# Sparse attention in a pinned order: softmax by single heads, out weight splits at named places, two transposes later, the last unit ahead of the next input

## The chip, the cores and the metric

The kernel runs on one core of a Trainium2 chip. Its time is device microseconds of one execution. Five engines work beside each other, each in its own instruction order: TensorE (PE: matmuls and transposes, into PSUM banks), VectorE (DVE), ScalarE (ACT), GpSimd (POOL) and SyncE (SP, which here issues nearly all loads). TensorE's clock is granted by a throttle; the profile gives it as a share of full speed (1.00 is 2.4 GHz, 0.50 is 1.2 GHz).

## The reference

Four layers over 256 tokens of width 1024, each x -> x + 1/2 FFN_a(x) -> x + Mixer(x) -> x + 1/2 FFN_b(x), every step between two RMS norms with a shift, scale and gate from a conditioning vector. Layers 0 and 3 have native sparse attention (NSA) as mixer, layer 1 stick-breaking and layer 2 differential attention. What matters here of the NSA mixer, for one block of 128 tokens:

```python
s = jnp.einsum('bqgrd,bngd->bgrqn', qb, k_cmp) * scale           # 15 compressed keys
p_cmp = jax.nn.softmax(where(valid, s - slopes * dist, NEG)) * valid
o_cmp = jnp.einsum('bgrqn,bngd->bqgrd', p_cmp, v_cmp)
...                                                             # the selected keys k_g, the window's keys kwb
p_sel = softmax(where(dist >= 0, s_sel - slopes * dist, NEG))
p_win = softmax(where(valid, s_win - slopes * d_int, NEG))
o = g[..., 0:1] * o_cmp + g[..., 1:2] * o_sel + g[..., 2:3] * o_win
return o.reshape(B, Q_BLK, NSA_QW) @ w_out
```

There are 16 heads in 4 groups. `k_cmp` and `v_cmp` come from a small two-layer network over windows of 32 tokens. With 256 tokens all four selection blocks are taken, and the window reaches over all tokens before, so both softmaxes run over all earlier tokens.

## The kernel before

All products are made in three passes of split single precision (hi x hi, lo x hi, hi x lo); each weight is loaded raw by SP (`raw_*`), cast to its high part on ACT (L135, `hi_*`) and its rest is made on DVE (L136, `lo_*`). Raw and split weights sit in rings of a few buffers, so a load waits until an older one has been used.

The NSA mixer is cut into named pieces, and the strings `plan` and `rest` give the order of the pieces. `run` calls them through `pin`, which lets the first TensorE instruction of a piece issue only after the last TensorE instruction of the piece before. So TensorE's order is that of the plan; the order on DVE, ACT and SP is decided by the scheduler from the order and the priorities in which the instructions are written.

There are four units: a (head groups 0 and 1, tokens 0 to 127), b (the same heads, tokens 128 to 255), c and d (groups 2 and 3, the two blocks of tokens). The pieces are:

- `gate`: the product p_g for the three gates, its tanh `gt` on ACT (L864) and its transposes `p_gt` (L867); `q gp part`: chunks of the query product in a bank `p_pr` with two halves, emptied to `qkv` by ACT (L774, even half) or DVE (L772, odd half); `kc`: keys and values for compression.
- `S u rp`: scores `p_s` (L915) of two heads of each of two groups (e is the group, rr the head) and their softmax: a score reduction on DVE (L920) that subtracts the distance and takes the maximum, for all eight rows of the pair; the maxima times the slope (L927); eight exponentials with sums (ACT, L933); reciprocal (L936) and the multiply by the gates (L937); eight multiplies `sc` (L943).
- `T u rp n`: four transposes `p_t` of the probabilities (L951) and a copy `pT` by ACT (L953); `P u rp n`: values times `pT` into the unit's bank `p_o` (L896).
- `hid k`: the first layer of the compression network, two loads `raw_cw` each; after `hid 3` its activation. `cout`: transposes `p_ht`, copy `hT` (L842), `p_kcT` and `p_vc`, which give the compressed keys and values.
- `C u`, `D u`, `E u`: the compressed branch: scores `p_sc` (L966) and softmax `pc`, transposes `p_t<-ident,pc` (L685) with their copies `pT` by ACT or DVE (L631), and the product `p_o<-pT,vc`. `put` moves `p_o` into `yh` and `yl` (L627, L628), the input of the out projection.
- `o h k n`: out projection of token block h with chunk k of the weights (`raw_wo`, `hi_wo`, `lo_wo`), for half n of the columns or both. `out_weight(k)` is called in `o`, where the chunk is first used.

Around it, the main loop calls `body` (the plan), then `post` for token block 0 (norm and residual, L371 to L377), `pre` (norm of the next step's input and its transposes `p_y`, L339), and then `tail` (the rest) with the work of token block 1. Score banks (`mm`) and transpose banks (`tp`) come in pairs, accumulators (`acc`) in fours.

Of the kernel before, what the change touches and what calls it, by code (L numbers as in the profile page):

```python
# [40 lines left out]
def trunk_kernel(ctx, tc, x, c, ada_w, ada_b, norm_g, ffn_w1, ffn_w2, nsa_w_in, nsa_cmp_pe, nsa_cmp_w1,  # L41
# [610 lines left out]
    def softmax_alibi(h, qk, sc, sl, nsl):  # L652


        K, n = 128 * (h + 1), len(qk[0])
        m = small([128, 2 * n], "sm_m")
        per = min(512 // K, n)
        for j0 in range(0, n, per):
            p = [bank("mm", [128, per, K], "p_s") for _ in range(2)]
            for j in range(per):  # L660
                for e in range(2):
                    qT, kT = qk[e][j0 + j]
                    nc.tensor.matmul(p[e][:, j, :], qT, kT[:, :K], start=True, stop=True)
# [28 lines left out]
    class Nsa(Mixer):  # L692
        W = D + 6 * 256 + 48
        plan = """gate; q 0 0; S a 0; q 0 2; S b 0 0; q 0 3; S b 0 1; kc 0 0; S a 1; T a 0 0; T a 0 1; kc 0 1; P a 0 0; P a 0 1;
                  kc 1 0; T b 0 0; T b 0 1; kc 1 1; P b 0 0; T b 0 2; P b 0 1; T b 0 3; q 1 4; P b 0 2; P b 0 3; S b 1 0;
                  q 1 5; S b 1 1; T a 1 0; T a 1 1; hid 0; P a 1 0; P a 1 1; S c 0; hid 1; hid 2; hid 3; T b 1 0; T b 1 1;
# [5 lines left out]
                  put d; o 1 0 1; o 1 1 1; o 1 2 1; o 1 3 1; o 1 4 0; o 1 5 0; o 1 6 0; o 1 7 0; o 1 4 1; o 1 5 1; o 1 6 1; o 1 7 1"""  # L702
# [60 lines left out]
        def q(self, gp, part):  # L763

            self.load_q(gp)
            for r in ((0, 1), (2, 3), (2,), (3,), (0,), (1,))[part]:
                if not r % 2:
                    self.pq = bank("acc", [128, 2, T], "p_pr")
                mm_w(self.pq[:, r % 2, :], self.w[gp], chunk(r))
                j = 4 * gp + r  # L770
                if r % 2:
                    nc.vector.tensor_scalar(self.qT[:, j, :], self.pq[:, 1, :], qscale[:, j:j + 1], None, op0=OP.mult)  # L772
                else:
                    nc.scalar.activation(self.qT[:, j, :], self.pq[:, 0, :], AF.Copy, scale=qscale[:, j:j + 1])  # L774
# [61 lines left out]
        def cout(self):  # L836
# [5 lines left out]
            nc.vector.tensor_copy(hT, p)  # L842
            self.kcmp = work.tile([128, 2, 2, 16], FT, name="kc", tag="kc", bufs=1)
# [15 lines left out]
        def gate(self):  # L859
# [4 lines left out]
            nc.scalar.activation(gt, p, AF.Tanh, scale=0.5)  # L864
            pt = bank("tp", [128, 2, 48], "p_gt")
            for h in range(2):
                nc.tensor.transpose(pt[:, h, :], gt[:, h * 128:(h + 1) * 128], ident[:48, :48])  # L867
            nc.vector.tensor_scalar(self.gates.rearrange("p h a b -> p h (a b)"), pt, 0.5, 0.5, op0=OP.mult, op1=OP.add)

        def o(self, h, k, n=None):  # L870
# [6 lines left out]
            if k not in self.wo:  # L877
                self.wo[k] = self.out_weight(k)
# [3 lines left out]
        class Attend:  # L882


            def __init__(self, nsa, gp, h):
                self.nsa, self.gp, self.h = nsa, gp, h
                self.tok, self.K = slice(h * 128, (h + 1) * 128), 128 * (h + 1)
                self.po, self.sc, self.m, self.t, self.ct = None, {}, {}, {}, {}
# [10 lines left out]
            def S(self, rp, r=None):  # L899
# [3 lines left out]
                if rs[0] == 0:  # L903
# [5 lines left out]
                    self.m[rp] = small([128, 2, 2, 2], "sm_m")  # L909
                sc, m = self.sc[rp], self.m[rp]  # L910
# [6 lines left out]
                for j, rr in enumerate(rs):  # L917
                    for e in range(2):
                        for b in range(2):
                            nc.vector.tensor_tensor_reduce(  # L920
                                out=sc[e][:, rr, b, :], in0=p[e][:, j, b, :], in1=dist[:, T - K:], scale=1.0,
                                scalar=-3.0e38, op0=OP.subtract, op1=OP.max, accum_out=m[:, e, rr, b:b + 1])
                if rs[-1] == 0:
                    return
                hd0 = 8 * gp + 2 * rp
                of = lambda t: t.rearrange("p (e r) -> p e r", e=2)[:, :, 2 * rp:2 * rp + 2]
                nc.vector.tensor_mul(m, m, of(nslope[:, 8 * gp:8 * gp + 8])[:, :, :, None].to_broadcast([128, 2, 2, 2]))  # L927
                l = small([128, 2, 2, 2], "sm_l")
                for rr in range(2):
                    for e in range(2):  # L930
                        for b in range(2):
                            o = sc[e][:, rr, b, :]
                            nc.scalar.activation(o, o, AF.Exp, bias=m[:, e, rr, b:b + 1], scale=slopes[hd0 + 4 * e + rr],  # L933
                                                 accum_out=l[:, e, rr, b:b + 1])
                r = small([128, 2, 2, 2], "sm_r")
                nc.vector.reciprocal(r, l)  # L936
                nc.vector.tensor_mul(r, r, self.nsa.gates[:, h, 8 * gp:8 * gp + 8, 1:3].rearrange(  # L937
                    "p (e r) b -> p e r b", e=2)[:, :, 2 * rp:2 * rp + 2, :])
                for b in range(2):
                    for e in range(2):  # L940
                        for rr in range(2):
                            o = sc[e][:, rr, b, :]
                            nc.vector.tensor_scalar(o, o, r[:, e, rr, b:b + 1], None, op0=OP.mult)  # L943

            def T(self, rp, n):
# [7 lines left out]
                nc.scalar.copy(t, p)  # L953
# [230 lines left out]
    with ExitStack() as st:  # L1184
# [4 lines left out]
        nc.gpsimd.iota(dist, pattern=[[-1, T]], base=128, channel_multiplier=1, allow_small_or_imprecise_dtypes=True)  # L1189
        nc.gpsimd.affine_select(out=dist, in_=dist, pattern=[[-1, T]], compare_op=OP.is_ge, fill=BIG, base=128,  # L1190
# [40 lines left out]
    for n, (i, s) in enumerate(subs):  # L1231
# [7 lines left out]
        gate = [] if last else list(pre(*subs[n + 1], 0))  # L1239
# [42 lines left out]
```

## Time and profile before

| | us |
|---|---|
| median of 3 runs (lowest, highest) | 2198.04 (2193.22, 2208.82) |
| the profiled execution, its span | 2198.95, 2197.2 |
| busy in the span: PE, DVE, ACT, POOL | 2105.5 (96%), 1621.3 (74%), 1117.9 (51%), 65.3 (3%) |
| mean granted clock | 0.984 |

The page shows TensorE as busy 96% of the span. A share over the whole span says little about two short stretches in it, so the rows below are read by stretch: windows give busy time and granted clock of each engine between two times; the waits say what an engine stood idle for; groups by line give mean durations; the timeline gives single instructions with the idle time before them in brackets.

### The profile page before, as it was taken

What the parts mean: (1) busy time and instruction counts of PE and PEld (TensorE: products, weight loads), DVE (VectorE), ACT (ScalarE), POOL (GpSimd) and SP (SyncE); (2) the same over time, 40 slices, a digit from 0 to 9 for tenths busy, and PEclk for the clock granted to TensorE, in tenths of its full rate; (3) what the DMA queues carried; (4) which work ended last, traced back from release to release, by engine and by line L of the source; (5) the groups of instructions that cost most, each with busy time, mean ns of one, the idle gap of its engine ahead of it and who ended that gap; (6) DMA issues with size and microseconds to landing.
All of it is one profiled execution on the core that took longest, in us unless ns stands there. A gap on an engine that the chain in (4) does not pass through costs nothing. (4 is left out here: it accounts for less than half of the span.)

```text
span 2197.2 us, 37373 instructions
## 1 busy us (share of the span) xinstructions
PE 2105.5 (96%) x14395; PEld 1864.4 (85%) x14395; DVE 1621.3 (74%) x2720; ACT 1117.9 (51%) x1989; POOL 65.3 (3%) x154
## 2 busy tenths in 40 slices
PE   5999898999999999999999999999999998998998
PEld 5999775899899978899999888799999987757998
DVE  7987866777798776777697858687778859556654
ACT  3454654644554456744464455654464436545443
POOL 1000000000000000000000000000000000000000
PEclk9999999999999999999999999999999999989999
DMA  9997752688699856388779948288869968524761
GB/s 313 338 349 269 253 135 72 195 291 271 198 330 307 285 189 217 114 291 274 247 259 310 319 162 278 70 266 284 265 206 335 314 200 260 130 70 157 245 202 59
DMA packets 338179, 512.55 MB, mean 233 GB/s; under 512 B 20832, under 2 KB 211256, under 8 KB 338000
## 3 DMA queue, kind: packets, MB, share of 16 engines
q1 hardware_dynamic: 329456, 501.15, 69.0%
q10 hardware_dynamic: 8544, 9.01, 1.4%
q8 instruction: 113, 1.85, 0.3%
q14 instruction: 66, 0.54, 0.1%
HBM read 507.91 MB, written 1.05 MB: 232 GB/s over the span
## 5 line engine op out<-in xcount | busy, mean ns | idle before, releaser
L135 ACT CAST hi_w<-raw_w 128x1024 fp32r<-128x1024 f32 x528 | 551.1, 1054 | 325.1 <-PE f L409 113.3
L136 DVE TENSOR_TENSOR lo_w<-raw_w,hi_w 128x1024 fp32r<-128x1024 f32 x528 | 631.8, 1220 | 102.6 <-ACT hi_w L135 94.4
L386 PE MATMUL p_gu<-yh,hi_w 128*128 128x256 f32 x2368 | 665.9, 281 | 4.0 <-DVE yh L351 4.0
L387 PE MATMUL p_gu<-yl,hi_w 128*128 128x256 f32 x2368 | 661.2, 279 | 0.3 <-DVE yl L352 0.3
L388 PE MATMUL p_gu<-yh,lo_w 128*128 128x256 f32 x2368 | 660.9, 279 | 0.0
L386 PEld LDWEIGHTS p_gu<-yh,hi_w 128*128 128x128 f32 x2368 | 445.8, 188 | 17.3 <-DVE lo_w L136 6.2
L192 DVE SCALAR_TENSOR_TENSOR ada_acc<-raw_ada,cT,ada_acc 128x512 f32<-128x512 f32 x500 | 373.8, 748 | 109.8 <-DMA raw_ada<-in_ada_w_dram 101.6
L387 PEld LDWEIGHTS p_gu<-yl,hi_w 128*128 128x128 f32 x2368 | 446.2, 188 | 5.4 <-issue 1.7
L388 PEld LDWEIGHTS p_gu<-yh,lo_w 128*128 128x128 f32 x2368 | 446.1, 188 | 0.0
L405 PE MATMUL f<-hi_w,hb 128*128 128x512 f32 x704 | 275.5, 392 | 3.1 <-ACT hb L550 3.1
L406 PE MATMUL f<-lo_w,hb 128*128 128x512 f32 x704 | 275.8, 392 | 0.0
L409 PE MATMUL f<-hi_w,hb 128*128 128x512 f32 x704 | 228.2, 391 | 0.0
L550 ACT CAST hb<-sg 128x256 fp32r<-128x256 f32 x148 | 60.2, 407 | 204.1 <-DVE sg L549 202.7
L548 ACT ACTIVATE sg<-p_gu 128x256 f32<-128x256 f32 x148 | 56.2, 380 | 201.1 <-PE p_gu L388 185.2
L405 PEld LDWEIGHTS f<-hi_w,hb 128*128 128x128 f32 x704 | 132.3, 188 | 30.0 <-ACT hb L550 5.2
L409 PEld LDWEIGHTS f<-hi_w,hb 128*128 128x128 f32 x704 | 131.5, 188 | 29.2 <-DVE hb L551 1.8
L406 PEld LDWEIGHTS f<-lo_w,hb 128*128 128x128 f32 x704 | 132.2, 188 | 24.5 <-issue 0.2
L549 DVE TENSOR_TENSOR sg<-sg,p_gu 128x256 f32<-128x256 f32 x148 | 61.5, 415 | 77.5 <-ACT sg L548 77.3
L551 DVE TENSOR_TENSOR hb<-sg,hb 128x256 fp32r<-128x256 f32 x148 | 62.4, 421 | 35.2 <-ACT hb L550 35.2
L350 ACT ACTIVATE y<-p_y,ab 128x128 f32<-128x128 f32 x184 | 67.2, 466 | 35.3 <-PE p_y L339 30.6
L387 PE MATMUL p_pr<-yl,hi_qk 128*128 128x256 f32 x256 | 71.8, 281 | 0.0
L386 PE MATMUL p_pr<-yh,hi_qk 128*128 128x256 f32 x256 | 71.5, 281 | 0.0
(274 smaller groups left out, 3203.0 us busy)
## 6 DMA issues: line engine op xcount, KB each, us to landing
raw_w<-in_ffn_w_dram SPq DMA_DIRECT2D x528, 512.0 KB
raw_ada<-in_ada_w_dram SPq DMA_DIRECT2D x288, 512.0 KB
raw_kv<-in_nsa_w_in_dram SPq DMA_DIRECT2D x16, 512.0 KB
raw_q<-in_nsa_w_in_dram SPq DMA_DIRECT2D x16, 512.0 KB
raw_cw<-in_nsa_cmp_w_dram SPq DMA_DIRECT2D x16, 512.0 KB
raw_wo<-in_nsa_w_out_dram SPq DMA_DIRECT2D x32, 256.0 KB
raw_qk<-in_sb_w_in_dram SPq DMA_DIRECT2D x16, 512.0 KB
raw_qk<-in_diff_w_in_dram SPq DMA_DIRECT2D x16, 512.0 KB
```

The costliest lines, as they stand in the source:

```text
L135: nc.scalar.copy(hi, src)
L136: nc.vector.tensor_sub(lo, src, hi)
L192: nc.vector.scalar_tensor_tensor(a, r[:, j], cT[:, k:k + 1], a, op0=OP.mult, op1=OP.add)
L350: nc.scalar.activation(y[:, j, :], p[:, j, :], AF.Identity, scale=ab[:, k:k + 1], bias=ab[:, 8 + k:9 + k])
L386: nc.tensor.matmul(o, cols(wh), yh[:, k, :], start=first and k == 0, stop=False)
L387: nc.tensor.matmul(o, cols(wh), yl[:, k, :], start=False, stop=False)
L388: nc.tensor.matmul(o, cols(wl), yh[:, k, :], start=False, stop=last and k == KC - 1)
L405: nc.tensor.matmul(acc[n], lh, wh[:, sl], start=first, stop=False)
L406: nc.tensor.matmul(acc[n], lh, wl[:, sl], start=False, stop=False)
L409: nc.tensor.matmul(acc[n], ll, wh[:, sl], start=False, stop=last)
L549: nc.vector.tensor_mul(sg, sg, p[:, 1, :])
L551: nc.vector.tensor_sub(hl[:, cc, :], sg, hh[:, cc, :])
```

## The change

- `gate` is cut in two: tanh in `gate`, transposes and their evacuation in `gate_T`, which stands behind `q 0 0`.
- `q` empties both halves of a `p_pr` bank after the second half's last matmul, and can run half of its rows (`q 1 4 0`, `q 1 4 1`, `q 1 3 0`, `q 1 3 1`).
- `cout` is cut in two (`cout`, `cout_T`), later in the plan and with other pieces between.
- `weight k` calls `out_weight(k)` at eight named places; its cast and subtraction are ordered behind the last copy `pT` on ACT.
- The softmax is made by single heads (one head of each of the two groups: four rows), the slope in the reduction itself, with tiles of four instead of eight maxima, sums and reciprocals. The distance constant changes its sign.
- The plan: C a and C b behind S c 1, S d 0 and S d 0 1 ahead of E a, D b directly ahead of E b, and the last part of unit d, with E d and `put d`, moves from `rest` into the plan, ahead of the next step's `pre`, which is pinned too.

```diff
-        plan = """gate; q 0 0; S a 0; q 0 2; ...
-                  ... hid 0; P a 1 0; P a 1 1; S c 0; hid 1; hid 2; hid 3; T b 1 0; T b 1 1;
-                  q 1 2; P b 1 0; T b 1 2; P b 1 1; T b 1 3; cout; C a; C b; q 1 3; P b 1 2; P b 1 3; S c 1;
-                  T c 0 0; T c 0 1; D a; P c 0 0; P c 0 1; E a; D b; S d 0 0; E b; o 0 0; o 0 1; S d 0 1; C c; o 0 2;
-                  T c 1 0; T c 1 1; o 0 3; P c 1 0; P c 1 1; D c; S d 1 0; E c; C d; S d 1 1; T d 0 0; T d 0 1; o 0 4;
-                  P d 0 0; T d 0 2; P d 0 1; T d 0 3; o 0 5; P d 0 2; P d 0 3; o 0 6; D d; o 0 7"""
-        rest = """E d; o 1 0 0; T d 1 0; T d 1 1; o 1 1 0; P d 1 0; T d 1 2; o 1 2 0; P d 1 1; T d 1 3; o 1 3 0; P d 1 2; P d 1 3;
-                  put d; o 1 0 1; ..."""
+        plan = """gate; q 0 0; gate_T; S a 0; q 0 2; ...
+                  ... hid 0; P a 1 0; P a 1 1; S c 0; hid 1; weight 0;
+                  hid 2; weight 1; hid 3; T b 1 0; T b 1 1; weight 2; q 1 2; P b 1 0; T b 1 2; weight 3; q 1 3 0; P b 1 1; T b 1 3; cout; q 1 3 1;
+                  P b 1 2; P b 1 3; cout_T; S c 1; C a; T c 0 0; T c 0 1; C b; P c 0 0; P c 0 1; S d 0 0; D a; weight 4;
+                  S d 0 1; E a; D b; weight 5; E b; o 0 0; C c; o 0 1; T c 1 0; T c 1 1; weight 6; o 0 2; P c 1 0; P c 1 1; S d 1 0;
+                  o 0 3; D c; weight 7; C d; S d 1 1; E c; T d 0 0; T d 0 1; o 0 4; P d 0 0; T d 0 2; o 0 5; P d 0 1; T d 0 3;
+                  o 0 6; P d 0 2; P d 0 3; o 0 7; D d; o 1 0 0; T d 1 0; E d; o 1 1 0; T d 1 1; P d 1 0; o 1 2 0; T d 1 2;
+                  P d 1 1; o 1 3 0; T d 1 3; P d 1 2; P d 1 3; put d"""
+        rest = """o 1 0 1; ..."""
...
+                if r % 2 and ks[-1] == KC - 1:
+                    j = 4 * gp + r
+                    nc.scalar.activation(self.qT[:, j - 1, :], self.pq[:, 0, :], AF.Copy, scale=qscale[:, j - 1:j])
                     nc.vector.tensor_scalar(self.qT[:, j, :], self.pq[:, 1, :], qscale[:, j:j + 1], None, op0=OP.mult)
...
+        def weight(self, k):
+            gate_on[:] = self.copied
+            self.wo[k] = self.out_weight(k)
+            gate_on[:] = []
...
                 for j, rr in enumerate(rs):
+                    heads = [8 * gp + 4 * e + 2 * rp + rr for e in range(2)]
...
                             nc.vector.tensor_tensor_reduce(
+                                out=sc[e][:, rr, b, :], in0=p[e][:, j, b, :], in1=dist[:, T - K:], scale=-slopes[heads[e]],
+                                scalar=3.0e38, op0=OP.add, op1=OP.min, accum_out=m[:, e, b:b + 1])
...
+                            nc.scalar.activation(o, o, AF.Exp, bias=m[:, e, b:b + 1], scale=-1.0, accum_out=l[:, e, b:b + 1])
+                    nc.vector.reciprocal(r, l)
+                    nc.vector.tensor_mul(r, r, self.nsa.gates[:, h, heads[0]:heads[1] + 1:4, 1:3])
...
-                nc.scalar.copy(t, p)
+                self.nsa.copied = [nc.scalar.copy(t, p).ins]
...
-        gate = [] if last else list(pre(*subs[n + 1], 0))
+        gate = []
+        if not last:
+            (pin if s == 1 and not i % 3 else lambda f: f())(lambda: gate.extend(pre(*subs[n + 1], 0)))
```

TensorE at the head of the plan, before; `p_g` is the gates' product, `p_gt` the transposes of its tanh, `p_pr` the query product:

```order
L387 MATMUL p_g<-yl,hi_gw 48x256
L388 MATMUL p_g<-yh,lo_gw 48x256
L867 MATMUL p_gt<-ident,gt 128x48 x2
L386 MATMUL p_pr<-yh,hi_q 128x256
L387 MATMUL p_pr<-yl,hi_q 128x256
```

And now, 48 query matmuls later:

```order
L387 MATMUL p_pr<-yl,hi_q 128x256
L388 MATMUL p_pr<-yh,lo_q 128x256
L877 MATMUL p_gt<-ident,gt 128x48 x2
L927 MATMUL p_s<-qkv 128x256 x4
L386 MATMUL p_pr<-yh,hi_q 128x256
```

The transposes have moved from the place ahead of the first query product to that between it and the first scores.

VectorE around E b, before; here L631 with `pT<-p_t` is the copy of the compressed probabilities that E b multiplies by, `ISA sc,sm_m` a score reduction:

```order
L631 COPY pT<-p_t 15x512
L927 TENSOR_TENSOR sm_m<-sm_m,nslope 128x8
L136 TENSOR_TENSOR lo_wo<-raw_wo,hi_wo 128x1024
L631 COPY pT<-p_t 15x512
L920 ISA sc,sm_m<-p_s,dist 128x256
```

VectorE ahead of that second copy now, with L944 the multiply of the reciprocals by the gates, L936 the score reductions and L948 the multiplies of `sc`; directly ahead of these rows stand the first copy L631, the last multiply of `pc`, a reciprocal (L943) and a subtraction `lo_wo` (L136):

```order
L944 TENSOR_TENSOR sm_r<-sm_r,gates 128x4
L936 ISA sc,sm_m<-p_s,dist 128x256
L936 ISA sm_m 128x1
L948 TENSOR_SCALAR sc<-sc,sm_r 128x256 x4
L936 ISA sc,sm_m<-p_s,dist 128x256
L936 ISA sm_m 128x1
L936 ISA sc,sm_m<-p_s,dist 128x256
L936 ISA sm_m 128x1
L936 ISA sc,sm_m<-p_s,dist 128x256
L936 ISA sm_m 128x1
L628 TENSOR_TENSOR yl<-p_o,yh 128x4x128
L631 COPY pT<-p_t 15x512
```

The second copy L631, that of D b, has moved from behind one multiply and one subtraction to behind a reciprocal, a subtraction, a multiply, four score reductions, four multiplies and L628.

TensorE at the end of the plan, before; `o_4071` is the out projection of token block 1, `p_y` the next step's input and `p_gx` its product:

```order
L896 MATMUL p_o<-pT,vc 64x512 x2
L405 MATMUL o_4071<-hi_wo,yh 128x512
L406 MATMUL o_4071<-lo_wo,yh 128x512
L409 MATMUL o_4071<-hi_wo,yl 128x512
L339 MATMUL p_y<-ident,xn 128x128 x8
L951 MATMUL p_t<-ident,sc 128x128 x4
```

And now, with `o_4057` the same out projection's first half of the columns and `o_4154` its second:

```order
L956 MATMUL p_t<-ident,sc 128x128 x4
L909 MATMUL p_o<-pT,qkv 64x256 x2
L405 MATMUL o_4057<-hi_wo,yh 128x512
L406 MATMUL o_4057<-lo_wo,yh 128x512
L409 MATMUL o_4057<-hi_wo,yl 128x512
L956 MATMUL p_t<-ident,sc 128x128 x4
L909 MATMUL p_o<-pT,qkv 64x256 x4
L339 MATMUL p_y<-ident,xn 128x128 x8
L405 MATMUL o_4154<-hi_wo,yh 128x512
```

All of unit d's transposes and value products now stand ahead of `p_y`, and the second half of the out projection stands directly behind it.

## Rows read from the trace of the kernel before

**Rows 1.** Windows: busy us (instructions) of each engine, granted clock, DMA share, GB/s.
```profile
253.40:403.20 149.80, 131.47 (x826) 95.72 (x826) 94.69 (x327) 78.59 (x222) 1.13 (x3) 0.93 0.42 121
403.20:1846.70 1443.50, 1418.56 (x9872) 1286.58 (x9870) 1102.34 (x1604) 750.29 (x1227) 45.46 (x64) 1.00 0.76 251
1846.70:2002.50 155.80, 138.60 (x826) 99.58 (x824) 95.16 (x325) 80.42 (x224) 1.10 (x2) 0.88 0.42 119
```

**Rows 2.** TensorE's waits, 253 to 404 us: us in total, times, longest.
```profile
PE p_o L896 <- ACT pT L953: 3.0, 3, 1.4
PE p_gt L867 <- ACT gt L864: 2.5, 1, 2.5
PE p_pr L386 <- ACT qkv L774: 2.2, 2, 1.6
PE p_ht L840 <- ACT hi_wo L135: 1.9, 1, 1.9
```

**Rows 3.** TensorE's waits, 1846 to 2003 us.
```profile
PE p_pr L386 <- ACT qkv L774: 3.0, 2, 2.4
PE p_o L896 <- ACT pT L953: 2.9, 2, 1.4
...
PE p_gt L867 <- ACT gt L864: 0.8, 1, 0.8
```

**Rows 4.** Windows by granted clock: one of seven at half speed, the seven's sum, one at full.
```profile
1952.70:1966.40 13.70, 12.82 (x39) 7.16 (x40) 6.49 (x31) 2.72 (x6) 0.00 (x0) 0.50 0.00 0
...
sum 57.90, PE 51.55 PEld 42.15 DVE 27.48 ACT 20.15 POOL 1.10; mean PE 7.36 PEld 6.02 DVE 3.93 ACT 2.88 POOL 0.16
...
334.80:382.60 47.80, 40.30 (x224) 23.63 (x223) 32.37 (x127) 25.32 (x77) 0.55 (x1) 1.00 0.18 56
```

**Rows 5.** Groups of VectorE, 253 to 404: busy us, mean ns of one | idle before.
```profile
L920 DVE CUSTOM_DVE_ANT_0 sc<-p_s,dist 128x256 f32<-128x256 f32 x32 | 12.0, 419 | 5.4 <-PE p_s L915 5.4
L136 DVE TENSOR_TENSOR lo_wo<-raw_wo,hi_wo 128x1024 fp32r<-128x1024 f32 x8 | 9.8, 1220 | 0.9 <-ACT hi_wo L135 0.9
L943 DVE TENSOR_SCALAR sc<-sc,sm_r 128x256 f32<-128x256 f32 x32 | 8.7, 348 | 0.0
...
L631 DVE COPY pT<-p_t 15x512 f32<-15x512 f32 x4 | 2.7, 679 | 3.0 <-PE p_t L685 2.9
L628 DVE TENSOR_TENSOR yl<-p_o,yh 128x512 fp32r<-128x512 f32 x4 | 2.7, 672 | 6.2 <-ACT yh L627 6.2
...
L936 DVE RECIPROCAL sm_r<-sm_l 128x8 f32<-128x8 f32 x8 | 1.6, 201 | 11.3 <-ACT sc L933 11.3
```

**Rows 6.** Timeline of ScalarE: start, us, instruction, count [idle before <- releaser].
```profile
255.51 0.38 ACT L864 ACTIVATE gt<-p_g 48x256 f32<-48x256 f32 x1 [2.56 <-DMA ada_c<-ada_r]
...
1852.05 1.05 ACT L135 CAST hi_kcvc<-raw_kcvc 128x1024 fp32r<-128x1024 f32 x1 [0.45 <-DMA raw_kcvc<-in_nsa_w_in_dram]
```

**Rows 7.** Timeline of SyncE's loads, and of ScalarE at the first out weight.
```profile
259.99 48.25 SPq L126 DMA_DIRECT2D raw_cw<-in_nsa_cmp_w_dram  x8
308.33 13.01 SPq L126 DMA_DIRECT2D raw_wo<-in_nsa_w_out_dram  x16
...
314.34 1.04 ACT L135 CAST hi_wo<-raw_wo 128x1024 fp32r<-128x1024 f32 x1 [3.62 <-DMA raw_wo<-in_nsa_w_out_dram]
```

**Rows 8.** Timeline of TensorE and ScalarE from the end of o 0 7.
```profile
376.75 0.40 PE L405 MATMUL o<-hi_wo,yh 128*128 128x512 f32 x1
376.99 0.40 PE L406 MATMUL o<-lo_wo,yh 128*128 128x512 f32 x1
377.65 0.60 ACT L371 ACTIVATE junk<-o 128x512 bf16<-128x512 f32 x1 [0.54 <-PE o L409]
383.89 1.94 PE L339 MATMUL p_y<-ident,xn 128*128 128x128 f32 x8 [4.16 <-DVE xn L355]
...
389.93 0.65 PE L896 MATMUL p_o<-pT,qkv 128*64 128x256 f32 x4
390.51 0.66 PE L951 MATMUL p_t<-ident,sc 128*128 128x128 f32 x4
```

More of the change, by code (lines that the diff above doesn't have):

```diff
@@ L693, in trunk_kernel @@
         W = D + 6 * 256 + 48
[L694 to L702 removed]
+        plan = """gate; q 0 0; gate_T; S a 0; q 0 2; S b 0 0; q 0 3; S b 0 1; kc 0 0; S a 1; T a 0 0; T a 0 1; kc 0 1;
+                  P a 0 0; P a 0 1; kc 1 0; T b 0 0; T b 0 1; kc 1 1; P b 0 0; T b 0 2; q 1 4 0; P b 0 1; T b 0 3; q 1 4 1;
+                  P b 0 2; P b 0 3; S b 1 0; q 1 5; S b 1 1; T a 1 0; T a 1 1; hid 0; P a 1 0; P a 1 1; S c 0; hid 1; weight 0;
+                  hid 2; weight 1; hid 3; T b 1 0; T b 1 1; weight 2; q 1 2; P b 1 0; T b 1 2; weight 3; q 1 3 0; P b 1 1; T b 1 3; cout; q 1 3 1;
[4 more added lines that the diff above has]
+                  P d 1 1; o 1 3 0; T d 1 3; P d 1 2; P d 1 3; put d"""
+        rest = """o 1 0 1; o 1 1 1; o 1 2 1; o 1 3 1; o 1 4 0; o 1 5 0; o 1 6 0; o 1 7 0; o 1 4 1; o 1 5 1; o 1 6 1; o 1 7 1"""
         def run(self, plan):
@@ L761, in load_q, with q @@
                     self.w[gp] += split_q(rows(nsa_w_in, self.lj * D * self.W + gp * 512, self.W, k0, 2, 512), "q")
-        def q(self, gp, part):
+        def q(self, gp, part, rows=None):
             self.load_q(gp)
-            for r in ((0, 1), (2, 3), (2,), (3,), (0,), (1,))[part]:
-                if not r % 2:
+            ks = range(KC) if rows is None else range(KC // 2 * rows, KC // 2 * (rows + 1))
+            for r in ((0, 1), None, (2,), (3,), (0,), (1,))[part]:
+                if not r % 2 and ks[0] == 0:
                     self.pq = bank("acc", [128, 2, T], "p_pr")
-                mm_w(self.pq[:, r % 2, :], self.w[gp], chunk(r))
-                j = 4 * gp + r
-                if r % 2:
+                mm_w(self.pq[:, r % 2, :], self.w[gp], chunk(r), ks)
+                if r % 2 and ks[-1] == KC - 1:
+                    j = 4 * gp + r
+                    nc.scalar.activation(self.qT[:, j - 1, :], self.pq[:, 0, :], AF.Copy, scale=qscale[:, j - 1:j])
                     nc.vector.tensor_scalar(self.qT[:, j, :], self.pq[:, 1, :], qscale[:, j:j + 1], None, op0=OP.mult)
-                else:
-                    nc.scalar.activation(self.qT[:, j, :], self.pq[:, 0, :], AF.Copy, scale=qscale[:, j:j + 1])
         def compress_in(self):
@@ L864, in gate, with gate_T @@
             nc.scalar.activation(gt, p, AF.Tanh, scale=0.5)
+            self.gt = gt
+        def gate_T(self):
+            gt = self.gt
             pt = bank("tp", [128, 2, 48], "p_gt")
@@ L932, in S @@
                             o = sc[e][:, rr, b, :]
[L933 to L941, printed above, removed]
+                            nc.scalar.activation(o, o, AF.Exp, bias=m[:, e, b:b + 1], scale=-1.0, accum_out=l[:, e, b:b + 1])
+                    nc.vector.reciprocal(r, l)
+                    nc.vector.tensor_mul(r, r, self.nsa.gates[:, h, heads[0]:heads[1] + 1:4, 1:3])
+                    for b in range(2):
+                        for e in range(2):
                             o = sc[e][:, rr, b, :]
-                            nc.vector.tensor_scalar(o, o, r[:, e, rr, b:b + 1], None, op0=OP.mult)
+                            nc.vector.tensor_scalar(o, o, r[:, e, b:b + 1], None, op0=OP.mult)
             def T(self, rp, n):
```

28 lines of the change are left out of this document (11 added, 17 removed).

## The prediction

> **What bounds the kernel now.** I read the windows first: TensorE's busy time and granted clock in four stretches of the profiled execution [rows 1]. The reader is to see that between 403.2 and 1846.7 us the clock is 1.00 and little is idle, and that the two stretches of the sparse-attention mixer (layers 0 and 3) are the exception: PE is idle for 149.80 - 131.47 = 18.3 us in the first and 155.80 - 138.60 = 17.2 us in the second, and the granted clock is 0.93 and 0.88. The order of instructions changes only inside these two stretches, so all of the gain and all of the loss has to come from there.
>
> Next I read what PE waits for in each [rows 2, 3]. The waits are short and named: the value products on the copy of the transposed probabilities (3.0 us), the gate transposes on the tanh (2.5), the second half of a query product on the evacuation of the first (2.2 and 3.0), the compression output on a weight cast (1.9). The longest single one is at the end: the next input's transposes start at 383.89 after a wait of 4.16 us, 6.2 us after ScalarE took up the finished output at 377.65 [rows 8].
>
> Last I read the clock. Seven stretches stand at 0.50 of full speed, which is the 1.2 GHz level: 57.9 us together, with PE busy in 51.55 of them [rows 4]. Work done at half speed takes twice as long, so they cost about 51.55 / 2 = 25.8 us. They begin behind the waits, but not behind each: 334.80 to 382.60 keeps 1.00 although PE is idle there for 47.80 - 40.30 = 7.5 us, while the same pieces of the plan in layer 3 fall to 0.50 at 1952.70 [rows 4]. In full: idle 35.5 us and 25.8 us of half speed, some 61 us that a better order could give at most.
>
> **The change part by part.** I take all 61.3 us out and walk the new order piece by piece with the durations of before, putting back every wait that I find.
>
> *Gate transposes behind the first query product.* They waited 2.5 and 0.8 us. The tanh of layer 0 starts only at 255.51, after ScalarE's queue sat 2.56 us behind a DMA [rows 6]; 48 query matmuls now lie in between, which is far longer, so the wait is gone.
>
> *Both halves of a query bank emptied after the second.* The wait between the halves goes (2.2 and 3.0 us), but the first scores, S a 0, now wait for both: only the two gate transposes lie between. One evacuation takes about 0.5 us, and casts queue ahead of it on ScalarE, such as the 1.05 us one at 1852.05 [rows 6]. I put back 2.05 us in layer 0 and 1.6 in layer 3: 3.7. Bounds: 0 each (evacuation at once, beside the transposes) and 3.0 each (the old wait).
>
> *Compression output in two pieces, with half a query product as cover.* Its wait of 1.9 us stood behind hi_wo casts; the first of these had itself waited 3.62 us for its data [rows 7], with the exponentials of the next scores queued behind it on ScalarE. The pieces between are half a query product each, so I take these waits as gone.
>
> *Out-weight splits at named places.* No instruction is added: the same 1.2 us subtraction on VectorE (L136) and 1.0 us cast on ScalarE (L135) move [rows 5, 7]. Gating them behind the last probability copy keeps them from overtaking it. The loads on SP's queue move too: eight compression loads were issued from 259.99 over 48.25 us, and the out-weight loads behind them [rows 7]; now two out-weight loads stand between compression loads, and the last compression load waits for a buffer that the first out-weight subtraction frees. I price this at 0.3 us per layer (the last compression product), with 0 as the lower bound; the upper one is the rival on the other side.
>
> *Softmax by single heads.* The multiply of the maxima goes, the reciprocal and the multiply by the gates double, on half the columns. A 128x8 reciprocal takes 201 ns [rows 5]; at that price for all three, a pair of heads costs VectorE 0.2 us more, 1.6 us over the 8 pairs of a layer. VectorE is busy 94.7 of 149.8 us [rows 1], so most of it hides. What it brings: the first exponential can start after four score reductions rather than eight, 4 x 0.42 = 1.7 us earlier on the 128x256 tiles [rows 5]. This takes away the waits of the transposes and of the value products behind q 1 2.
>
> *C a and C b behind S c 1, S d 0 1 earlier, D b directly ahead of E b.* Here are the new waits. C a needs a score bank that the reductions of S c 1 free: 1.5 us per layer. D a (0.95), S d 0 1 (1.1), S d 1 1 (1.0) and o 0 4 (0.8) each wait for a bank or a VectorE result. P a 1, P c 0, P d 0 and T d 1 0 together wait 1.7. The worst is E b. It multiplies by the copy of what D b has just transposed, and that copy (L631, on VectorE) stands in VectorE's order behind a reciprocal 0.20, an out-weight subtraction 1.22, a multiply 0.2, a reduction 0.42, four multiplies 4 x 0.35, three reductions 3 x 0.42 and a product's remainder 0.67; with its own 0.68 that is 6.0 us by the mean durations [rows 5], and 5.6 as I take it, since such rows overlap by some 0.06 us each. By my walk VectorE enters this row 2.1 us before PE reaches E b, so PE waits 3.5 us, in each layer. Behind it stand o 0 0, C c and everything else of PE. Bounds: 0, if VectorE is that much ahead, and 5.6.
>
> *The last unit ahead of the next input.* After o 0 7 there used to be only E d and one product; now the chain of 6.2 us [rows 8] is covered. Twelve output products at a pitch of 0.24 us (376.75 to 376.99) make 2.9 us, four sets of transposes at 0.66 and four sets of value products at 0.65 make 5.2 [rows 8]: 8.1 us, without D d and E d. The wait of 4.2 us is gone in both layers, 8.3 us.
>
> The sum of the new waits: 3.7 for S a 0; per layer 0.3 + 1.5 + 0.95 + 1.1 + 1.0 + 0.8 + 1.7 + 3.5 = 10.85, twice 21.7; together 25.4. By their bounds they lie between about 15 and 34.
>
> *The clock.* With the waits that preceded them gone, I expect the half-speed stretches at the head, in the middle and at the tail to go. The wait at E b, longer than any now in the middle, should bring one back in each layer. An average one costs 25.8 / 7 = 3.7 us, the one at 1952.70 costs 12.82 / 2 = 6.4 [rows 4]; I take 4.5 each, 9 together. Bounds: none, and all 25.8.
>
> **The sum** is made against the profiled execution, 2198.95 us (span 2197.2), which lies 0.9 us over the median of 2198.04: 2198.95 - 35.5 - 25.8 + 25.4 + 9 = 2172.05. **2172 us**, 1.2% faster.
>
> **Rivals.**
> *The clock stays up in the middle.* The stretch from 334.80 kept 1.00 through waits of this kind, the one at 1952.70 did not [rows 4]. Without the 9 us: 2163.
> *The clock stays down in the second half of both layers.* Many short waits on banks could keep it at 1.2 GHz: 1952.70 is a case of it, 334.80 to 382.60 speaks against [rows 4]. With 30 us of PE work per layer at half speed, 15 each, 30 replaces the 9: 2193. The Trainium skill has this as a rule ("TensorE: Matmul & The Clock Gate", "A second HAM failure mode: psum-queue depth-cycling"): a kernel whose TensorE idles briefly and often between groups of matmuls that cycle through PSUM banks sees the clock go down and up again and again. By that rule this case would be the likely one; the trace bears it out at one of the two places only, so I give it the smaller chance.
> *The idle only moves.* If VectorE's and ScalarE's own orders set the pace, the waits I took out come back downstream. VectorE is busy for two thirds of the stretch from 334.80 (32.37 of 47.80 us), not all of it [rows 4], which speaks against. With the 7.5 us of idle of that stretch kept in both layers, and half of the 2.5 + 0.8 + 2.2 + 3.0 - 3.7 = 4.8 us won at the head lost: 2172 + 15 + 2.4 = 2189.
> *Slower: the last compression load is late.* SP's queue is in order; if the load that waits for the first out-weight subtraction comes late, PE stands still at hid 3, each microsecond of delay costing one per layer, and the compressed branch hangs on it. It turns the forecast's 27 us into a loss of over 22 from (27 + 22) / 2 = 24.5 us per layer on. The eight loads took 48 us at 6 us apart [rows 7], so one or two steps (6 to 12 us) would give 2184 to 2196; more than four steps are needed for slower, at some 2222.
>
> **How the numbers follow.** About 1% (22 us) is what a measurement of this kernel can tell from no change. Forecast 0.50, no slow clock 0.22, slow clock in the second half 0.14, idle only moves 0.08, late load 0.06. The forecast's own range is 2164 to 2182; 2176 is the bound of "faster", and about 0.36 of its 0.50 lies below. With 0.21 of the second case faster is 0.57; slower takes 0.05 from the late load and the worst of the two cases before it; the rest, 0.38, is the same within 1%. The range for 8 in 10 runs from 15 us of new waits and no slow clock (2198.95 - 61.3 + 15 = 2152.7) to the second rival: 2152 to 2194.
>
> **What would show it.** The waits of p_gt on gt, p_pr on qkv, p_ht on hi_wo and p_y on xn are gone; the first p_s waits about 2 us; the compressed product p_o waits about 3.5 us on the VectorE copy pT (L631) in each layer, and the clock falls to 0.50 shortly after, once per layer; the half-speed stretches add up to some 20 us instead of 57.9. The stretches from the gate to the next input get shorter by about 12 us in layer 0 and 15 in layer 3. The forecast is wrong if a wait over 6 us stands at hid 3, if half speed fills most of the output products, or if the wait at E b isn't there.

## The result and the profile after

The changed kernel takes 2175.25 us (2169.74 to 2176.5, 4 runs) against 2196.34 for the kernel before in the same comparison: a ratio of 0.9889, interval 0.9846 to 0.9931. A second set of 6 runs on another occasion (e6 below) gave 2170.88 and 0.9881 (0.9859 to 0.9903). The forecast was 2172. The profiled execution is the fastest of the first four, 2169.74 us with a span of 2167.9; the runs scatter by 7 us, which must be kept in mind with every difference below.

Windows of the changed kernel, cut at the same places as [rows 1] (from the end of the gates' product to the end of the out projection, in both layers): busy us and instructions of each engine, granted clock, DMA share, GB/s.

```profile
253.10:395.20 142.10, 133.78 (x825) 96.22 (x824) 93.63 (x335) 79.05 (x221) 1.23 (x3) 0.92 0.44 123
395.20:1836.60 1441.40, 1418.17 (x9875) 1285.41 (x9874) 1104.92 (x1605) 751.29 (x1227) 45.74 (x64) 1.00 0.76 252
1836.60:1973.20 136.60, 128.02 (x824) 92.30 (x823) 94.10 (x332) 80.50 (x224) 1.10 (x2) 0.96 0.47 132
```

The stretches are 7.7 and 19.2 us shorter, and what lies between is 2 us shorter. TensorE's order between them is unchanged; there one stretch at half speed is 6.8 us long (1384.8 to 1391.6) where it was 10.3 before (1392.9 to 1403.2), which is worth 1.7 us. TensorE's idle time in the two stretches is 142.10 - 133.78 = 8.3 and 136.60 - 128.02 = 8.6 us, where it was 18.3 and 17.2. In this execution the clock rose in layer 3 alone (0.96 for 0.88); in layer 0 it is as low as before (0.92 for 0.93), so what layer 0 gained is idle time. TensorE's waits in the first stretch (us in total, times, longest):

```profile
PE p_o L909 <- DVE pT L631: 2.5, 1, 2.5
PE p_s L927 <- ACT qkv L775: 1.7, 1, 1.7
PE p_sc L971 <- DVE sm_m L936: 1.5, 1, 1.5
PE p_hid L824 <- DMA raw_cw<-in_nsa_cmp_w_dram: 1.0, 1, 1.0
PE p_gate L281 <- DVE peT L785: 0.7, 1, 0.7
PE p_o L909 <- ACT pT L958: 0.6, 1, 0.6
```

In the second stretch E b and C a wait 2.5 and 1.5 us again, and further down stand:

```profile
PE p_hid L824 <- DMA raw_cw<-in_nsa_cmp_w_dram: 1.3, 1, 1.3
PE p_o L909 <- ACT pT L958: 0.9, 2, 0.6
...
PE p_s L927 <- ACT qkv L775: 0.7, 1, 0.7
PE p_t L685 <- DVE pc L985: 0.3, 1, 0.3
PE p_s L927 <- DVE qkv L776: 0.2, 1, 0.2
```

No wait of [rows 2, 3] on gt, hi_wo or qkv in the query product is left. The worst is the new one at E b. The timeline of TensorE and then of VectorE shows it:

```profile
340.53 1.05 PE L685 MATMUL p_t<-ident,pc 128*15 128x128 f32 x8
344.10 1.31 PE L909 MATMUL p_o<-pT,vc 15*64 15x512 f32 x2 [2.52 <-DVE pT L631]
```

```profile
339.05 0.18 DVE L943 RECIPROCAL sm_r<-sm_l 128x4 f32<-128x4 f32 x1
339.14 1.21 DVE L136 TENSOR_TENSOR lo_wo<-raw_wo,hi_wo 128x1024 fp32r<-128x1024 f32 x1
340.27 0.15 DVE L944 TENSOR_TENSOR sm_r<-sm_r,gates 128x4 f32<-128x4 f32 x1
340.34 0.42 DVE L936 CUSTOM_DVE_ANT_0 sc<-p_s,dist 128x256 f32<-128x256 f32 x1
...
340.68 1.14 DVE L948 TENSOR_SCALAR sc<-sc,sm_r 128x256 f32<-128x256 f32 x4
...
342.77 0.68 DVE L628 TENSOR_TENSOR yl<-p_o,yh 128x512 fp32r<-128x512 f32 x1
343.37 0.67 DVE L631 COPY pT<-p_t 15x512 f32<-15x512 f32 x1
```

The eight transposes of D b are done at 341.6; the copy that E b needs starts at 343.37, behind a row that VectorE works off from 339.05 without a pause. At the end of the plan the wait of 4.16 us in [rows 8] is gone:

```profile
384.53 1.40 PE L909 MATMUL p_o<-pT,qkv 128*64 128x256 f32 x8
385.86 1.09 PE L339 MATMUL p_y<-ident,xn 128*128 128x128 f32 x8
386.71 0.48 PE L405 MATMUL o<-hi_wo,yh 128*128 128x512 f32 x1
```

Last the clock. Of [rows 4]'s 57.9 us at half speed 34.2 are left in the two stretches, in five windows: four in layer 0 and one in layer 3. Below stand the two that begin shortly ahead of or behind E b, and the sum over all five; the other three begin at the head (3.4 us from 261.8), behind C a (6.8 from 330.1) and at 364.2 (3.4).

```profile
343.70:354.00 10.30, 9.90 (x28) 7.03 (x29) 5.56 (x18) 1.43 (x4) 0.00 (x0) 0.50 0.16 53
...
1924.10:1934.40 10.30, 10.30 (x34) 8.13 (x32) 4.26 (x16) 2.07 (x5) 0.00 (x0) 0.50 0.16 52
sum 34.20, PE 33.80 PEld 25.27 DVE 20.77 ACT 14.08 POOL 0.00; mean PE 6.76 PEld 5.05 DVE 4.15 ACT 2.82 POOL 0.00
```

### The profile page after: what moved, and what is told of

It is laid out like the page before. It is cut to its first block, busy times and chain, and to the rows that moved or that the text cites. A ratio compares the mean times of both kernels' runs of the same rounds, so it can differ in the third digit from the quotient of the medians.

```text
span 2167.9 us, 37376 instructions
## 1 busy us (share of the span) xinstructions
PE 2096.4 (97%) x14395; PEld 1856.1 (86%) x14395; DVE 1622.9 (75%) x2736; ACT 1119.8 (52%) x1989; POOL 67.3 (3%) x154
## 4 chain that ended last, share of the span: by engine, by line
PE 74%; DVE 11%; issue 5%; DMA 5%; ACT 4%; POOL 2%; ACTq 0%; SPq 0%; DVEq 0%; POOLq 0%
PE p_gu L386 12%; PE p_gu L388 12%; PE p_gu L387 12%; PE f L405 6%; PE f L406 6%; PE f L409 6%; DVE lo_w L136 3%; DMA raw_ada<-in_ada_w_dram 3%; PE p_o L909 1%; PE p_pr L386 1%; PE p_pr L387 1%; PE p_pr L388 1%; PE p_t L956 1%; POOL rx L325 1%; PE o L405 1%
## 5 line engine op out<-in xcount | busy, mean ns | idle before, releaser
L136 DVE TENSOR_TENSOR lo_w<-raw_w,hi_w 128x1024 fp32r<-128x1024 f32 x528 | 633.1, 1221 | 103.6 <-ACT hi_w L135 97.2
L409 PEld LDWEIGHTS f<-hi_w,hb 128*128 128x128 f32 x704 | 131.6, 188 | 29.3 <-DVE hb L551 1.9
L406 PEld LDWEIGHTS f<-lo_w,hb 128*128 128x128 f32 x704 | 132.2, 188 | 24.5 <-DVE lo_w L136 0.3
```

What stands on the lines that cost most here:

```text
L136: nc.vector.tensor_sub(lo, src, hi)
L406: nc.tensor.matmul(acc[n], lh, wl[:, sl], start=False, stop=False)
L409: nc.tensor.matmul(acc[n], ll, wh[:, sl], start=False, stop=last)
```

## The experiments

The idle time is that of TensorE in the two stretches together, length less busy time of the windows; the half speed is worked out from their granted clock as 2 x (1 - clock) x length. The clock is given in hundredths, so such a sum is good to some 3 us (windows at 0.50 add up to 20.4 for e1). Both are read from one profiled execution of each kernel, which can be its slowest (e8, e10, e11). Ratios are to the kernel before on the same occasion (e1 to e4, e5 to e8 and e9 to e11 stand side by side).

| kernel | median us | ratio (interval) | idle us | half speed us |
|---|---|---|---|---|
| before | 2196.34 | 1 | 35.5 | 58 |
| the change | 2175.25 | 0.9889 (0.9846, 0.9931) | 16.9 | 34 |
| e1 both copies of D b on ScalarE | 2163.01 | 0.9848 (0.9828, 0.9868) | 15.6 | 20 |
| e2 tail undone | 2189.64 | 0.9960 (0.9943, 0.9977) | 29.3 | 54 |
| e3 softmax by pairs | 2177.97 | 0.9914 (0.9892, 0.9936) | 22.5 | 34 |
| e4 head undone | 2175.47 | 0.9901 (0.9883, 0.9920) | 21.7 | 31 |
| e5 no named places | 2171.59 | 0.9882 (0.9860, 0.9903) | 18.7 | 33 |
| e6 the change again | 2170.88 | 0.9881 (0.9859, 0.9903) | 18.5 | 25 |
| e7 compression loads first | 2166.46 | 0.9858 (0.9835, 0.9880) | 17.0 | 28 |
| e8 e1 and all short waits covered | 2167.11 | 0.9857 (0.9831, 0.9883) | 10.4 | 39 |
| e9 e1 and e7 | 2163.39 | 0.9846 (0.9827, 0.9865) | 12.6 | 27 |
| e10 e9 and the head covered | 2160.98 | 0.9823 (0.9801, 0.9846) | 9.9 | 33 |
| e11 the tail alone, on before | 2182.70 | 0.9929 (0.9912, 0.9946) | 25.2 | 47 |

**e1: the wait at E b.**

```diff
-                self.ct[e] = transpose4(lambda rr: self.pc[:, 4 * e + rr, :], e)
+                self.ct[e] = transpose4(lambda rr: self.pc[:, 4 * e + rr, :], 1 if self.gp == 0 and self.h else e)
```

> The changed kernel with one thing altered: both copies behind D b are made by ScalarE, where the first one stood on VectorE behind the long row. In the changed kernel's profile PE waits 2.5 us at E b in each layer, and a half-speed stretch begins behind it (343.7 to 354.0 with PE busy 9.90, 1924.1 to 1934.4 with 10.30). Theory: the wait is the cause of both; it falls to some 0.9 us and the half-speed stretches go with it, 2 x 1.6 + 4.95 + 5.15 = 13 us less: 2162. Rival one: the clock falls from the row of short waits around it, not from this one; the wait shrinks and the half speed stays: 2172. Rival two: the wait moves on to o 0 0, which needs L628 from the same VectorE row: 2175, no change.

It took 2163.01 us. The timelines of TensorE and of ScalarE in this kernel:

```profile
341.24 1.05 PE L685 MATMUL p_t<-ident,pc 128*15 128x128 f32 x8
342.95 1.54 PE L909 MATMUL p_o<-pT,vc 15*64 15x512 f32 x4 [0.66 <-ACT pT L631]
```

```profile
341.83 0.51 ACT L942 ACTIVATE sc<-sc,sm_m 128x256 f32<-128x256 f32 x1
...
342.34 1.03 ACT L631 COPY pT<-p_t 15x512 f32<-15x512 f32 x2
```

One exponential stands ahead of the copies, and E b waits 0.7 us instead of 2.5 in both layers; o 0 0 follows without a wait. Windows of the two stretches:

```profile
253.40:393.40 140.00, 131.64 (x824) 95.06 (x823) 93.38 (x335) 79.58 (x223) 1.10 (x2) 0.94 0.44 125
1833.90:1966.50 132.60, 125.39 (x823) 89.79 (x822) 93.26 (x330) 80.16 (x224) 1.10 (x2) 0.99 0.48 136
```

The second stretch has a clock of 0.99 now, the first 0.94: of the half speed that I hung on this wait one of two went. In layer 3 none stands behind E b; in layer 0 6.8 us are left (345.2 to 352.0) of 10.3. The theory's number (2162) was met, its half speed only in part. By the medians the time fell by 8 to 12 us, by the ratios, which allow for the occasion, by 7 to 9, with intervals that overlap; the wait alone is 3.6 of them. So the change had a price here that one expression in the code takes back.

**e2 and e11: the tail.** In e2 the old end of the plan is put back in the changed kernel. In e11 the kernel before gets the last unit ahead of the next input and nothing else: its pieces stand in their old order (E d directly behind o 0 7), where the change also rearranges them. Each edit also takes away or adds the pinning of `pre`; the move and the pinning were not tried apart.

```diff
-                  ... P d 0 3; o 0 7; D d; o 1 0 0; T d 1 0; E d; o 1 1 0; ... P d 1 2; P d 1 3; put d"""
-        rest = """o 1 0 1; ...
+                  ... P d 0 3; D d; o 0 7"""
+        rest = """E d; o 1 0 0; T d 1 0; T d 1 1; o 1 1 0; ... P d 1 2; P d 1 3; put d; o 1 0 1; ...
...
-            (pin if s == 1 and not i % 3 else lambda f: f())(lambda: gate.extend(pre(*subs[n + 1], 0)))
+            gate.extend(pre(*subs[n + 1], 0))
```

> The changed kernel with the end of the plan undone: unit d's last part, E d and put d stand behind the next step's norm and transposes again, which are not pinned. Theory: the wait of p_y on xn comes back with 4.2 us in each layer, and with it the half-speed stretch behind it (PE busy 4.76 and 7.37 us at half speed before, 2.4 and 3.7 lost): 8.4 + 6.1 = 14.5 us more, 2190. Rival one: the wait returns but the clock does not fall behind it: 2183. Rival two: most of the tail's gain came from what stands in front, and the last unit hides it anyway: 2175 to 2178.

> The kernel before with the end of the plan alone changed: unit d's last part, E d and put d ahead of the next step's norm and transposes, these pinned; all else as before. Theory: the tail is worth the same alone as in the changed kernel, where undoing it cost 14 to 18 us: the waits of 4.2 us go, with about 6 us of half speed: 2182. Rival: alone it gains less, since without single heads and named weights the last value products and transposes wait in front of it: 2188 to 2191. If it is 2182, the tail makes up most of the whole change's 22 to 27 us.

e2 took 2189.64, e11 2182.70: undoing it costs 0.0075 of the time (16 us), and it gives 0.0071 (16 us) alone. In e2 the wait of p_y is back, in its old length in both layers, and with it half speed beside it (381.0 to 387.9 and 1971.7 to 1981.9; 54 us in all against 34):

```profile
PE p_y L339 <- DVE xn L355: 4.2, 1, 4.2
...
PE p_t L956 <- ACT y L350: 0.7, 1, 0.7
```

So the theory holds on both sides: the tail is worth 14.5 us as worked out, a little more by the times, and it makes up some two thirds of the whole change. It doesn't need the other parts.

**e3: softmax by pairs.**

```diff
+                    self.m[rp] = small([128, 2, 2, 2], "sm_m")
...
-                    m = small([128, 2, 2], "sm_m")
...
+                if rs[-1] == 0:
+                    return
+                l = small([128, 2, 2, 2], "sm_l")
...
+                nc.vector.reciprocal(r, l)
```

> The changed kernel with the softmax by pairs again: the slope stays in the reduction, but all eight reductions come ahead of the first exponential, and one reciprocal and one multiply serve eight rows. Theory: the waits of the value products on the probabilities come back, at most the 3.0 and 2.9 us of before, and in part the half speed behind them: 5.9 us, with one half-speed stretch of 5 us per layer at most: 2181 to 2191. Rival one: the pieces put in as cover (half a query product, the later weights) have taken these waits away, not the single heads: 2175. Rival two: VectorE saves 0.2 us a pair, 1.6 us a layer, and since E b waits for VectorE this is time won: 2172.

2177.97 us; against the two values of the change that is 0.0025 to 0.0033 more (5 to 7 us), with intervals that overlap. The idle time grew by 4 to 6 us, but not where I had it: the value products wait for the probabilities only 0.7 us in layer 0. Two of its waits there are:

```profile
PE p_hid L824 <- DMA raw_cw<-in_nsa_cmp_w_dram: 3.1, 2, 2.9
...
PE o L409 <- DVE yl L628: 1.7, 1, 1.7
```

The last compression load comes later (how is shown at e7), while E b waits 1.1 us instead of 2.5. Theory and rivals each have a part of it: the cover did take the old waits away, VectorE's row ahead of E b is shorter, and what single heads bring comes from elsewhere. The gain is small and not told from none by the times.

**e4: the head undone.**

```diff
-        plan = """gate; q 0 0; gate_T; S a 0; ...
+        plan = """gate; gate_T; q 0 0; S a 0; ...
...
-                if r % 2 and ks[-1] == KC - 1:
-                    j = 4 * gp + r
+                if ks[-1] != KC - 1:
+                    pass
+                elif r % 2:
```

> The changed kernel with the head undone: the gate transposes ahead of the first query product, and the first half of a query bank emptied as soon as it is done. Theory: the waits of before return, 2.5 + 0.8 at the gate and 2.2 + 3.0 in the query product, for the 1.7 + 0.9 that the first scores wait now: 5.9 us, and half speed at the head moves from one stretch (3.4 us) to two (3.4 each): 1.7 us more; 2182 to 2183. Rival: the first scores need the evacuations either way and the time lost ahead of them is won behind them: 2175 to 2177.

2175.47 us, 0.0012 to 0.0020 more than the change, which is inside the intervals: the rival's number. In the profile the gate's wait is back, the query's is not:

```profile
PE p_gt L880 <- ACT gt L873: 3.4, 1, 3.4
...
PE p_pr L386 <- ACT qkv L779: 0.6, 1, 0.6
```

With 1.7 and 0.9 us in layer 3 that makes 6.6 us of waits at the head for 2.6 in the changed kernel, 4 us and not 5.9. So the 5.2 us of the query product in [rows 2, 3] went away for the most part without the late evacuation; which of the other parts did it was not tried.

**e5, e6 and e7: named places and the order of the loads.** e5 writes each split in `o` again; e6 is the changed kernel; e7 moves two places:

```diff
-                  ... S c 0; hid 1; weight 0; hid 2; weight 1; hid 3; T b 1 0; T b 1 1; weight 2; q 1 2;
+                  ... S c 0; hid 1; hid 2; hid 3; weight 0; T b 1 0; weight 1; T b 1 1; weight 2; q 1 2;
```

> The changed kernel without the named places: each out-weight split is written in the out projection that uses it first, as before, and is not ordered behind a probability copy; all eight compression loads stand ahead of the out-weight loads again. Theory: the casts overtake copies on ScalarE again, and waits of the kind of before return (1.9 us of p_ht on a cast, and up to 1.4 us of the value products), 3 to 4 us per layer, while the waits for the compression loads (1.0 and 1.3 us) go: about 5 us more, 2180, with up to 5 us of half speed above. Rival one: the other covers (half a query product between the pieces) are enough, and only the loads' waits go: 2173. Rival two: E b waits less, since the out-weight subtraction in VectorE's row ahead of it stands elsewhere: 2165 to 2170.

> The changed kernel itself once more, beside the others of this call, so that they stand against runs of the same chip: 2175, between 2169 and 2178. If the runs scatter by more than 5 us, the rivals of e3 and e4 can't be told from it by their times and are to be read from their waits.

> The changed kernel with the first two out-weight splits named behind the last compression product, so that SyncE issues all eight compression loads ahead of the out-weight loads. Theory: the wait of the compression product for its load (1.0 and 1.3 us) comes from the two out-weight loads between them and goes: 2173. Rival one: the load waits for a buffer and not for its place in the queue: the wait stays, 2175. Rival two: the later casts meet the copies of P b and the compression output and cost more than is won: 2177 to 2180.

e5 is as fast as the change (2171.59 and 2170.88): the named places bring nothing by themselves that the times show. In its profile the waits for the loads are gone and E b waits 1.7 us, but C a waits 3.0. e7 is 4.4 us faster, more than the theory's 2, with intervals that overlap. SyncE's loads in the changed kernel, its first out-weight subtraction on VectorE and its last compression load by itself; then the last compression load of e7:

```profile
304.44 1.11 SPq L126 DMA_DIRECT2D raw_wo<-in_nsa_w_out_dram  x2
305.65 2.37 SPq L126 DMA_DIRECT2D raw_cw<-in_nsa_cmp_w_dram  x2
...
306.40 1.23 DVE L136 TENSOR_TENSOR lo_wo<-raw_wo,hi_wo 128x1024 fp32r<-128x1024 f32 x1 [0.34 <-ACT hi_wo L135]
...
307.65 0.37 SPq L126 DMA_DIRECT2D raw_cw<-in_nsa_cmp_w_dram  x1
```

```profile
306.48 0.37 SPq L126 DMA_DIRECT2D raw_cw<-in_nsa_cmp_w_dram  x1
```

In the changed kernel the last compression load is issued at 307.65, and the subtraction ends at 306.40 + 1.23 = 307.63. The two stand 0.02 to 0.03 us apart in layer 3, in e1, in e3 and in e6 as well; in e3 the subtraction starts at 308.43 and the load at 309.68. So the last load waits for the buffer that the first out-weight subtraction frees, as the prediction said; the place behind two other loads held up only the load before it. In e7 no subtraction stands ahead of it: it is issued at 306.48, as soon as the first compression product has ended (304.50 + 1.95 = 306.45), and the product's wait of 1.0 to 1.8 us is gone. e7's edit takes away both the place in the queue and the wait for the subtraction, so that the product's wait went doesn't prove the theory: rival one had the cause right (a buffer) and the outcome wrong (that the wait stays). The rest of the 4.4 us is half speed or scatter.

**e8, e9 and e10: towards a better version.** e9 joins e1 and e7; e10 adds the first line below, e8 both.

```diff
-        plan = """gate; q 0 0; gate_T; S a 0; q 0 2; S b 0 0; ...
+        plan = """gate; q 0 0; gate_T; q 0 2 0; S a 0; q 0 2 1; S b 0 0; ...
...
-                  P b 1 2; P b 1 3; cout_T; S c 1; C a; T c 0 0; T c 0 1; C b; ...
+                  P b 1 2; cout_T; S c 1; P b 1 3; T c 0 0; C a; T c 0 1; C b; ...
```

> The kernel of e1 with the other waits of the changed kernel covered too: half a query product between the gate transposes and the first scores (1.7 and 0.9 us), all compression loads first (1.0 and 1.3), and a value product and a set of transposes between the scores of S c 1 and C a (1.5 us each), some 7.9 us of waits, of which 2 should be left. Theory: idle and half speed go together; 2163 - 6 - 5 = 2152. Rival one: only the idle goes: 2157. Rival two: the covered pieces shift VectorE's and ScalarE's rows, above all that ahead of E b, and as much returns there: 2163.

> The two single edits that were faster than the changed kernel, together: both copies behind D b on ScalarE (e1), and all compression loads ahead of the out-weight loads (e7). They touch different waits, 2.5 to 0.7 us at E b and 1.0 to 1.9 at the compression product per layer, so they should add up: 6 to 7 us of idle less than the changed kernel, and the half speed behind E b. Theory: 2158, between 2154 and 2162. Rival: the half-speed stretches that e1 lost come by chance at one place or another, and only the idle goes: 2164 to 2167.

> As the kernel of e9, with half a query product between the gate transposes and the first scores as well. In the changed kernel the first scores waited 1.3 to 3.0 us in layer 0 and 0.7 to 1.4 in layer 3, for ScalarE and VectorE; 1.4 us of query product covers half of it. Theory: 2 to 3 us less than e9, 2155. Rival one: the exponentials of the first scores come later by as much and the wait moves to the first transposes: the same as e9. Rival two: as in e8, which had fewer waits and more half speed in the middle, it comes out at 2165: then it is the order at the head that makes the middle slow, and not the pieces around C a.

e9 is no faster than e1, so the two gains don't add up; its 2163.39 lies between the theory (up to 2162) and the rival (from 2164). Against e7, the copies on ScalarE bring 3 us here, with intervals that overlap. e10 has the lowest median of all, 2160.98 us and a ratio of 0.9823, 0.6% or 13 us better than the change; its interval ends at 0.9846, where that of the first measurement of the change begins, and below that of the second. From e1 and e9 the times don't tell it. e8 has as little idle time as e10, 10.4 us, and is slower. TensorE in e8 at D a, and the windows of the half speed that follows in both layers:

```profile
331.84 1.05 PE L685 MATMUL p_t<-ident,pc 128*15 128x128 f32 x8 [1.91 <-DVE pc L985]
```

```profile
333.10:350.20 17.10, 17.10 (x45) 9.06 (x45) 8.63 (x31) 5.59 (x17) 0.00 (x0) 0.50 0.12 40
1916.90:1934.00 17.10, 17.10 (x47) 9.21 (x46) 8.32 (x28) 5.55 (x17) 0.00 (x0) 0.50 0.11 33
```

The wait at C a (1.5 us) had become one of 1.9 at D a, and the clock then stayed at 1.2 GHz for 17 us in which TensorE was never idle. e10, without that edit, keeps the wait at C a and has 6 us less half speed, in an execution that was its slowest (2167.3 us). e8's second rival, something returning near E b, gave the better number; what came back there is not idle time but clock. That the edit at C a is the cause is likely, not shown: the two intervals overlap.

One thing more stands in e10's profile, E b in both layers and the windows of half speed behind it:

```profile
339.38 1.85 PE L909 MATMUL p_o<-pT,vc 15*64 15x512 f32 x4 [0.66 <-ACT pT L631]
...
1920.05 2.15 PE L909 MATMUL p_o<-pT,vc 15*64 15x512 f32 x4 [0.66 <-ACT pT L631]
```

```profile
340.50:350.70 10.20, 10.20 (x31) 8.10 (x31) 4.16 (x13) 2.49 (x8) 0.00 (x0) 0.50 0.16 53
...
1920.90:1931.10 10.20, 10.20 (x32) 7.71 (x30) 4.44 (x13) 2.23 (x7) 0.00 (x0) 0.50 0.20 62
```

E b waits only 0.7 us, as in e1, and still 10.2 us of half speed follow in each layer, as long as behind the wait of 2.5; in e9 it is 6.9 and 6.8 us (341.9 to 348.8 and 1918.9 to 1925.7). So half speed behind E b doesn't need a long wait there, and e1's theory of its cause is not borne out. Why it stayed away in layer 3 of e1 is open.

## Why the prediction was right, and where its terms were not

The sum was 2198.95 - 35.5 - 25.8 + 25.4 + 9 = 2172. Measured in the profiled execution it reads 2198.95 - 35.5 - 25.8 + 16.9 + 16.9 = 2171.5, and it took 2169.74; the 1.7 us of half speed that went between the two stretches are the rest. The prediction had let all of the gain come from inside them. Two terms of the sum were off by 8 us each, with opposite signs: the mechanisms of the waits were right, but that the sum came within 2.3 us is luck.

- *The old waits go.* Right for all of them: gt, qkv in the query product, hi_wo, hT, and xn at p_y. e2 and e11 show the tail's share by itself at its size. Not all causes were right: the query product's waits also go without the late evacuation (e4), and those of the value products without single heads (e3).
- *New waits, 25.4 us.* Measured 16.9. C a was 1.5 as forecast, E b 2.5 for 3.5: VectorE's row ran from 339.05 to 344.04, 5.0 us for 5.6, and had begun 2.5 us ahead for 2.1. S a 0 was 2.6 in sum for 3.7. The mis-sized term is that of D a, S d 0 1, S d 1 1 and o 0 4, 7.7 us in sum, of which 0.3 came. The prediction names no row for these four, and no run shows why they were too high; I believe that in walking the order I let each piece wait for its bank from a late start that an earlier wait of mine had made. The value products and T d 1 0 were 1.5 for 3.4. The load ahead of the last compression product had the right mechanism, the buffer that the subtraction frees, and was under-sized, 1.0 and 1.3 us for 0.3.
- *The clock, 9 us.* Measured 33.80 / 2 = 16.9. The half speed behind E b came in both layers and near the size forecast, (9.90 + 10.30) / 2 = 10.1 us for 9. What also came were the three stretches of layer 0 at the head, behind C a and at 364.2, 13.6 us long, which I had expected to go with the waits. The reason given for the half speed at E b, that this wait is longer than any now in the middle, is not borne out: e9 and e10 have it behind a wait of 0.7 us.
- *By layer:* 7.7 and 19.2 us for 12 and 15; in e6, the same kernel, 137.70 and 137.80 us long, so 12.1 and 18.0.
- *The rivals.* "The clock stays down in the second half of both layers" did not come, with 34 us at half speed for its 60. "The idle only moves" did not come either: 16.9 of 35.5 us are left. "Slower by a late load" was right in its mechanism and named its place, hid 3, but the delay was 1 to 2 us where 24.5 would have decided.

What stays open is when the clock falls. It isn't set by the sum of the idle time: e8 and e10, with 10 us of it, had 39 and 33 us of half speed, and e1, with 15.6, had 20. The Trainium skill ties such swings to brief idling between groups of matmuls ("TensorE: Matmul & The Clock Gate", "A second HAM failure mode: psum-queue depth-cycling"); that the clock is 0.50 from 343.7 to 354.0 and 1.00 ahead of it and behind agrees with it, but within these kernels less of that idling did not mean less half speed.

## What to carry to other kernels

When an order is written by hand for one engine, look at what stands on the other engines ahead of each small result that the engine waits for: here giving one copy behind a 5 us row of VectorE to ScalarE was worth 7 to 9 us, as much as the single heads (5 to 7, not told from none) and the named places (nothing that shows) together. Work of the present step that doesn't depend on the next one's norm belongs ahead of its transposes: that was two thirds of the gain, in one edit and without the rest. And judge an edit that shortens waits by the time, not by the idle time: two versions with 10 us of idling in some 275 had medians 6 us apart, and one with 16 us as fast as the better of them to within 2.

## What the runs showed of the hardware that I had not expected

The same kernel falls to half speed at different places from one execution to the next. In the first profiled execution of the change the two stretches stand at clocks of 0.92 and 0.96, in the second (e6, below) at 0.96 and 0.95:

```profile
253.40:391.10 137.70, 128.12 (x824) 92.15 (x823) 93.57 (x335) 79.29 (x221) 1.10 (x2) 0.96 0.45 127
1833.60:1971.40 137.80, 128.92 (x824) 92.47 (x823) 94.29 (x332) 81.23 (x224) 1.10 (x2) 0.95 0.46 131
```

In the second, layer 0 has half speed behind E b alone, and layer 3 has some behind C a that the first did not have (1908.2 to 1918.4). TensorE's idle time is nearly the same in both (16.9 and 18.5 us), and its order is the same; the half speed is 34 and 25 us. That is 4 to 5 us of time, of the order of the scatter of the runs (2167.47 to 2174.39 in e6), and as much as the smaller parts of this change are worth. And the wait of the first scores in layer 0, with the same code at the head, was 1.7 us in the change, 1.3 in e6, 2.4 in e1 and 3.0 in e7, which the order of the plan doesn't tell either.
